# Block 2's mixer: v ahead of lx, masks built earlier, the scale of z moved, GpSimd relieved

## The chip, the cores and the metric

The kernel runs on one core of one Trainium2 chip. The metric is the device time of one execution in microseconds (us). The engines are called PE (TensorE), DVE (VectorE), ACT (ScalarE), POOL (GpSimd) and SP (SyncE, which issues most transfers).

## The reference

Two transformer blocks run one after the other on 256 tokens of 1024 channels in fp32. Block 1 is a hybrid mixer with a mixture of 32 experts. Block 2, which the change is in, has a mixer of a gated linear recurrence (lru) and a gated linear attention (gla), and then a feed-forward part:

```python
h = rms_norm(x, norm1[l]); p = h @ w_in[l]
lru_x, lru_g, q, k, v, g, z = jnp.split(p, SPLIT_IDX, axis=-1)
lru_x = causal_depthwise_conv_2(lru_x, conv_w[l], conv_b[l])      # 4 taps
r = sigmoid(block_diag(lru_x, w_a) + b_a); i = sigmoid(block_diag(lru_x, w_i) + b_i)
log_a = -LRU_C * r * softplus(-lam); a = exp(log_a)
u = sqrt(-expm1(2 * log_a)) * (i * lru_x)                          # then h = a * h + u
lru_o = rg_lru * gelu(lru_g)
log_alpha = log_sigmoid(z @ w_alpha + b_alpha) / GATE_TAU
# chunks of 64: bcum = cumsum(log_alpha); k_dec = k * exp(b_end - bcum)
# q_dec = q * exp(b_end); o = (q @ k_dec^T) @ v + q_dec @ state
gla_o = rms_norm(o, gla_norm) * silu(g)
x = x + concat(lru_o, gla_o) @ w_out
```

Channels: lru_x, lru_g, v and g have 512 each, q and k 256, z 16.

## The kernel before

A matrix product in fp32 is made of three products of rounded halves. A weight tile of 128 by 1024 arrives by DMA (raw); ACT writes its high half (hi), then DVE or POOL subtracts and writes its low half (lo); PE computes high by high, low by high, high by low. Activations are split the same way once.

Block 2's mixer is a list of units, each a weight tile with its 24 products (12 wide ones for v), worked through by `run_units`. For unit i it emits in this order: the actions of `at_pre(i)`, the split of unit i+2, the matmuls of unit i, the action that takes up the result of unit i-1, and the actions of `at(i)`. So each engine's order is fixed by this emission, and each engine works its own list strictly in order. `later(n, f)` puts f at the current unit plus n, `soon` in front of the current unit's actions.

The units are: 0 z, 1 and 2 k, 3 and 4 q, 5 to 8 lru_x (named lx, with the convolution behind it), 9 to 12 v, 13 to 16 lru_g (lg), 17 to 20 g, 21 to 28 the eight row products with w_out. The low halves of units 6 to 14 are made by POOL (`P2`).

The tokens' norm scale (rsb, a row of 256 scales on all partitions) isn't known when the first units begin; their unscaled results wait in PSUM. The sums of squares of h (sh) and of h times gain (g, sum sg) are taken on ACT. At unit `SCALE` a chain of 16 small operations on DVE gives the scale, then dg, a diagonal matrix, and PE multiplies it by ones (rsp) so that ACT can copy rsb. Everything with `from_scale` follows then.

From z come zb (product with w_alpha and bias), its softplus by an exponential and a polynomial of nine steps on DVE (L400), the running sum (`la`), and the decays of k and q (kd, qd). `gate_mm` multiplies a convolved tile xf by the block-diagonal masks wab (built from w_a and w_i), `gate_act` applies the sigmoids (rg, ix) and multiplies ix by xf. `lru_exp` makes al and the tanh from rg, `lru_q` and `lru_u` the input of the recurrence's scan. `k_turn` transposes kd, `scores` and `update` make the score tiles sT and the states st, `attend` the attention output, `gla_norm` its norm, on POOL.

Block 1's weights stream before all this, and the feed-forward part of block 2 follows.

Of the kernel before, what the change touches and what calls it, by code (L numbers as in the profile page):

```python
# [69 lines left out]
def kernel(ctx: ExitStack, tc: tile.TileContext, *aps, dbg=None, stage=9):  # L70
# [154 lines left out]
    def late_loads():  # L225
# [9 lines left out]
        loads += [(wal, A["gla_w_alpha_2"][0]), (wz2, wcols("w_in_2", 2560, 16))]  # L235
# [231 lines left out]
    loads2 = deque([("kq", 1024), ("lx", 0), ("v", 1536), ("lg", 512), ("g", 2048), (("wo", 0), 0), (("wo", 1), 0)])  # L467
# [659 lines left out]
    with ExitStack() as pp:  # L1127
# [317 lines left out]
    with ExitStack() as pc:  # L1445
# [36 lines left out]
        SCALE = 5  # L1482


        wab = [mw.tile([128, 4, 128], F32, name=f"wab{i}", tag=f"wab{i}") for i in range(2)]
        diag = mw.tile([128, 128], F32, name="diag")
        cmask = mw.tile([128, T], F32, name="cmask")

        def masks():
            for t, src_ in zip(wab, (wa2, wi2)):  # L1490
                V.memset(t, 0.0)
                for s in range(2):
                    r = slice(s * 64, (s + 1) * 64)
                    V.tensor_copy(t[r, :, r], src_[r])

        def chunks():
            V.memset(diag, 0.0)
            for s in range(2):
                V.memset(diag[s * 64:(s + 1) * 64, s * 64:(s + 1) * 64], 1.0)
            V.memset(cmask, 1.0)  # L1500
            V.memset(cmask.rearrange("p (c t) -> p c t", c=4)[:, :, 0:1], 0.0)

# [11 lines left out]
        def after_lx(t):  # L1514
            def f(o):
# [17 lines left out]
                later_pre(2, gate_mm, t)  # L1533
# [509 lines left out]
```

## Time and profile before

| | |
|---|---|
| median of three runs | 1029.76 us (1028.13, 1030.2, 1029.76) |
| profiled execution | 1031.31 us, of which span 1029.5 us |
| granted TensorE clock, mean share | 0.911 |
| PE busy | 872.9 us, 85% of the span |
| DVE busy | 433.3 us, 42% |
| ACT busy | 318.8 us, 31% |
| POOL busy | 147.5 us, 14% |
| block 2's mixer | 708.8 to 833.5 us |

The shares are means over stages with different limits. Durations below are those of the one profiled execution; busy PE time at a clock of 0.50 is work that takes half as long at 1.00.

### The profile page before, as it was taken

The numbers are of one execution on the slowest core, as the hardware profiler recorded it, in microseconds if no ns is written. First come the engines' busy times: TensorE is split into PE (matmuls) and PEld (weight loads), VectorE is DVE, ScalarE is ACT, GpSimd is POOL, SyncE is SP. The second block draws the span as 40 slices with busy tenths as digits, with TensorE's granted clock in tenths as the row PEclk, the third lists the DMA queues.
The fourth block names the chain that finished last, engine by engine and source line by source line (L and its number), as shares of the span: only waits on it lengthen the run. The fifth ranks groups of instructions, "written<-read, shape, count | busy, mean of one in ns | idle before, by whom it ended". The sixth has DMA issues, their size and how long they took to land.

```text
span 1029.5 us, 13573 instructions
## 1 busy us (share of the span) xinstructions
PE 872.9 (85%) x5631; PEld 616.6 (60%) x5632; DVE 433.3 (42%) x756; ACT 318.8 (31%) x533; POOL 147.5 (14%) x127
## 2 busy tenths in 40 slices
PE   8999998999868597665858667689679999999997
PEld 8988887777414141321414123136659789999996
DVE  6898565553101110100101010016896776555554
ACT  6665453434001100000000000005446545444444
POOL 4232024002000000000000000002452223111112
PEclk9999998999878778887887878799889999999999
DMA  9594424366999999998999999999725345474301
GB/s 292 135 388 174 164 91 156 96 231 266 393 428 423 427 428 414 427 422 344 429 427 428 427 428 412 428 412 383 273 81 185 102 162 167 164 246 161 126 1 42
DMA packets 77392, 287.85 MB, mean 280 GB/s; under 512 B 12499, under 2 KB 41358, under 8 KB 65678
## 3 DMA queue, kind: packets, MB, share of 16 engines
q1 hardware_dynamic: 76486, 285.03, 71.0%
q0 software_dynamic: 592, 1.60, 0.4%
q8 instruction: 46, 0.75, 0.3%
q10 hardware_dynamic: 248, 0.30, 0.1%
q14 instruction: 20, 0.16, 0.0%
HBM read 285.87 MB, written 1.05 MB: 279 GB/s over the span
## 4 chain that ended last, share of the span: by engine, by line
PE 35%; DMA 10%; DVE 6%; ACT 1%; issue 1%; POOL 0%; DVEq 0%; ACTq 0%; SPq 0%; POOLq 0%
PE p L1185 6%; PE mm L339 5%; PE mm L341 5%; PE mm L340 5%; DMA raw<-in_w_gate_dram 4%; PE py L1211 3%; DMA raw<-in_w_down_dram 3%; PE po L309 3%; PE po L311 3%; PE po L310 3%; PE gp L1168 2%; DMA rawx<-in_w_down_dram 2%; DMA raw<-in_w_up_dram 1%; DVE za L400 1%; DVE xf L1529 1%
## 5 line engine op out<-in xcount | busy, mean ns | idle before, releaser
L339 PE MATMUL mm<-hnh,hi 128*128 128x256 f32 x808 | 233.4, 289 | 1.2 <-ACT cx L702 0.6
L341 PE MATMUL mm<-hnh,lo 128*128 128x256 f32 x808 | 228.6, 283 | 1.4 <-DVE lo L330 1.4
L340 PE MATMUL mm<-hnl,hi 128*128 128x256 f32 x808 | 228.1, 282 | 0.0
L1185 PE MATMUL p<-raw,xse 128*32 128x512 f32 x1008 | 158.1, 678 | 62.8 <-DMA raw<-in_w_gate_dram 57.0
L330 DVE TENSOR_TENSOR lo<-raw,hi 128x1024 fp32r<-128x1024 f32 x137 | 168.9, 1237 | 79.8 <-ACT hi L329 79.8
L329 ACT ACTIVATE hi<-raw 128x1024 fp32r<-128x1024 f32 x152 | 159.1, 1058 | 100.0 <-PE mm L340 39.8
L339 PEld LDWEIGHTS mm<-hnh,hi 128*128 128x128 f32 x808 | 153.6, 190 | 10.6 <-issue 7.5
L341 PEld LDWEIGHTS mm<-hnh,lo 128*128 128x128 f32 x808 | 153.6, 190 | 2.4 <-DVE lo L330 2.2
L340 PEld LDWEIGHTS mm<-hnl,hi 128*128 128x128 f32 x808 | 153.9, 190 | 0.9
L1185 PEld LDWEIGHTS p<-raw,xse 128*32 128x32 f32 x1008 | 36.8, 123 | 172.1 <-issue 85.4
L1211 PE MATMUL py<-raw,hs 128*32 128x512 f32 x496 | 86.4, 719 | 36.3 <-DMA raw<-in_w_down_dram 30.4
L1250 DVE TENSOR_TENSOR h<-h,pc 128x512 f32<-128x512 f32 x32 | 20.5, 683 | 138.2 <-PE pc L1248 138.2
L1211 PEld LDWEIGHTS py<-raw,hs 128*32 128x32 f32 x496 | 19.2, 128 | 95.2 <-DMA raw<-in_w_down_dram 44.5
L1375 POOL TENSOR_TENSOR g<-h,gain 128x512 f32<-128x512 f32 x2 | 3.5, 1779 | 472.3 <-DVE h L1250 472.3
L1168 PE MATMUL gp<-oh,xnf 128*128 128x128 f32 x256 | 65.8, 432 | 4.8 <-ACT xse L1175 4.8
L1168 PEld LDWEIGHTS gp<-oh,xnf 128*128 128x128 f32 x256 | 62.2, 334 | 6.7 <-ACT xse L1175 6.7
L1239 DVE SCALAR_TENSOR_TENSOR lo<-py,gs,hi 128x512 fp32r<-128x512 f32 x14 | 10.5, 751 | 111.5 <-ACT hi L1238 110.8
L1928 POOL TENSOR_TENSOR sgf<-sgf,rsb 128x256 f32<-128x256 f32 x22 | 31.7, 1441 | 134.4 <-ACT sgf L1927 134.4
L1192 ACT ACTIVATE sg<-p 128x512 f32<-128x512 f32 x8 | 4.8, 599 | 146.4 <-PE p L1185 136.0
L330 POOL TENSOR_TENSOR lo<-raw,hi 128x1024 fp32r<-128x1024 f32 x15 | 37.3, 2495 | 40.3 <-ACT hi L329 40.3
L1238 ACT ACTIVATE hi<-py,gs 128x512 fp32r<-128x512 f32 (+1 forms) x15 | 10.1, 673 | 102.5 <-PE py L1211 102.2
L1202 ACT ACTIVATE hs<-p 128x512 f32<-128x512 f32 x8 | 4.8, 597 | 112.7 <-PE p L1200 112.7
(472 smaller groups left out, 1138.3 us busy)
## 6 DMA issues: line engine op xcount, KB each, us to landing
raw<-in_w_gate_dram SPq DMA_DIRECT2D x32, 2048.0 KB
raw<-in_w_up_dram SPq DMA_DIRECT2D x31, 2048.0 KB
raw<-in_w_down_dram SPq DMA_DIRECT2D x28, 2048.0 KB
raw<-in_w_in_dram SPq DMA_DIRECT2D x14, 2048.0 KB
raw<-in_w_ffn_in_dram SPq DMA_DIRECT2D x22, 1024.0 KB
raw<-in_w_out_dram SPq DMA_DIRECT2D x6, 2048.0 KB
raw<-in_w_ffn_out_dram SPq DMA_DIRECT2D x5, 2048.0 KB
raw<-in_w_down_dram SPq DMA_DIRECT2D x12, 512.0 KB
```

Of the source, the lines that this page charges most:

```text
L309: P.matmul(po[a, j], yh[:, ts], wh[:, 0, ns], start=(i == 0), stop=False)
L310: P.matmul(po[a, j], yh[:, ts], wl[:, 0, ns], start=False, stop=False)
L311: P.matmul(po[a, j], yl[:, ts], wh[:, 0, ns], start=False, stop=end)
L329: S.activation(hv[:, r], src[:, r], AF.Copy)
L330: lo_on[0].tensor_tensor(lv, src, hv.bitcast(F32), op=ALU.subtract)
L339: P.matmul(o, wh, xh, start=first, stop=False)
L340: P.matmul(o, wh, xl, start=False, stop=False)
L341: P.matmul(o, wl, xh, start=False, stop=last)
L1168: P.matmul(p[:, kk, :], xn[:, a, 4 * hf + kk::8], OT[g][:, a, :], start=(a == 0), stop=(a == 1))
L1185: P.matmul(p[r], XS[g][:, k, r], ew(4 * g + i, m, k), start=(k == 0), stop=(k == 7))
L1211: P.matmul(PY[g][n][r], HT4[g][:, f, r], ew(4 * g + i, "d", f)[:, n * 512:(n + 1) * 512], start=(f == 0), stop=(f == 3))
L1928: G.tensor_tensor(t, t, rsb, op=ALU.mult)
```

## The change

- The v units come ahead of the lx units, in the loads and in the list: 5 to 8 are v, 9 to 12 lx.
- No low half is made on POOL any more (`P2` is gone). The products ix by xf, the product in `lru_u`, and half of the products h by gain move from POOL to DVE, the square of al to ACT.
- DVE makes the sums of squares of g for the second 128 tokens; ACT scales the rows of h at the end of the scale chain (`rows2_`), which DVE did.
- The masks wab, diag and cmask are built by DVE in `pools2`, during the experts' stage of block 1, in a pool of their own, and not at units 1 and 6.
- z's row scale is applied behind its second product: `after_z` copies 48 rows (high and low parts, w_alpha stacked twice), the product runs at unit 4, and DVE multiplies by rsb when it forms zb. The bias goes into ACT's Abs and is added again in `la`.
- `SCALE` is 6 (was 5), `KT` 14 (was 13), and most actions behind it one unit later. The four `lru_exp` stand at unit 16 together (were two at 14, two at 15), the four scans at 19. The convolved tiles' gates come three units after (was two); the decay's exponentials come one unit after `la` (was two), with the load of the sigmoid's table behind them (it was ahead of the polynomial).

```diff
-P2 = (4, 5, 6, 7, 8, 9, 10, 11, 12)
-KT = 13
+KT = 14
...
-    loads2 = deque([("kq", 1024), ("lx", 0), ("v", 1536), ("lg", 512), ("g", 2048), (("wo", 0), 0), (("wo", 1), 0)])
+    loads2 = deque([("kq", 1024), ("v", 1536), ("lx", 0), ("lg", 512), ("g", 2048), (("wo", 0), 0), (("wo", 1), 0)])
...
                 combine(g, a, n, tag)
-                if not a:
-                    G.tensor_tensor(X2["g"][:, a, ns], h[:, a, ns], gains[1][:, ns], op=ALU.mult)
+                V.tensor_tensor(X2["g"][:, a, ns], h[:, a, ns], gains[1][:, ns], op=ALU.mult)
...
-                V.tensor_scalar(h[:, a, :], X2["g"][:, a, :], y1[:, a:a + 1], None, op0=ALU.mult)
+                S.activation(h[:, a, :], X2["g"][:, a, :], AF.Copy, scale=y1[:, a:a + 1])
...
+        def sums_g1():
             for n in range(2):
-                ns = slice(n * 512, (n + 1) * 512)
-                V.tensor_tensor(X2["g"][:, 1, ns], h[:, 1, ns], gains[1][:, ns], op=ALU.mult)
+                x = X2["g"][:, 1, n * 512:(n + 1) * 512]
+                V.scalar_tensor_tensor(xf.rearrange("p a t -> p (a t)")[:, :512], x, 1.0, x, op0=ALU.mult, op1=ALU.mult,
+                                       accum_out=X2["sg"][:, 1, n:n + 1])
...
-                later_pre(2, gate_mm, t)
+                later_pre(3, gate_mm, t)
...
-            G.tensor_tensor(ix[:, t, :], ix[:, t, :], xf[:, t, :], op=ALU.mult)
+            V.tensor_tensor(ix[:, t, :], ix[:, t, :], xf[:, t, :], op=ALU.mult)
...
-                G.tensor_tensor(s2, al, al, op=ALU.mult)
+                S.activation(s2, al, AF.Square)
...
-            G.tensor_tensor(s2, s2, ix, op=ALU.mult)
+            V.tensor_tensor(s2, s2, ix, op=ALU.mult)
...
         def after_z(o):
-            z1 = za[:16, 0, :]
-            V.tensor_tensor(z1, o[32:48], rsb[32:48], op=ALU.mult)
-            V.tensor_tensor(zs, o[:16], rsb[:16], op=ALU.mult)
-            V.tensor_tensor(zs, zs, z1, op=ALU.add)
-            later_pre(1, zf)
+            S.activation(zs, o[:48], AF.Copy)
...
         def zexp():
+            V.tensor_tensor(zb, Z["p"], rsb[:, None, :].to_broadcast([128, 2, T]), op=ALU.mult)
             for j in range(2):
-                V.tensor_scalar(zb[:, j, :], Z["p"][:, j, :], cols2[:, c_gb + j:c_gb + j + 1], None, op0=ALU.add)
-            S.activation(zu, zb, AF.Abs)
+                S.activation(zu[:, j, :], zb[:, j, :], AF.Abs, bias=cols2[:, c_gb + j:c_gb + j + 1])
             S.activation(zu, zu, AF.Exp, scale=-1.0)
-            S.activation(small.tile([128, 1], F32, name="one"), ones[:, 0:1], AF.Sigmoid)
...
-            later(2, lambda: [S.activation(za, za, AF.Exp, scale=1.0 / 16),
-                              S.activation(eb.unsqueeze(3), be, AF.Exp, scale=1.0 / 16)])
-            later(2, kq_decay)
+            later(1, lambda: [S.activation(za, za, AF.Exp, scale=1.0 / 16),
+                              S.activation(eb.unsqueeze(3), be, AF.Exp, scale=1.0 / 16),
+                              S.activation(small.tile([128, 1], F32, name="one"), ones[:, 0:1], AF.Sigmoid)])
+            later(3, kq_decay)
...
-        units += [col_unit(src2("lx"), t * 128, after_lx(t), tag="mm" if t else "op") for t in range(4)]
         units += [v_unit(i) for i in range(4)]
+        units += [col_unit(src2("lx"), t * 128, after_lx(t)) for t in range(4)]
...
-            at_pre(17 + hd // 2, attend, hd)
+            at_pre(18 + hd // 2, attend, hd)
...
         for t in range(4):
-            at(14 + t // 2, lru_exp, t)
-        at(16, lru_q)
-        at(17, lru_u)
+            at(16, lru_exp, t)
+        at(17, lru_q)
+        at(18, lru_u)
...
-        run_units(units, ready=early2, pool=lambda i: i in P2)
+        run_units(units, ready=early2)
```

Three places of the engines' orders show what the diff doesn't. The first is DVE on the way to the first gate product, which needs xf. Before, from zb on (za by zu is the polynomial; rg is lx times rsb, xf by rg are the convolution's taps):

```order
L1614 TENSOR_SCALAR zb<-tp,cols_141 128x256 x2
L1521 TENSOR_TENSOR rg<-mm,rsb 128x256
L1529 SCALAR_TENSOR_TENSOR xf<-rg,cols_141,xf 128x255
L1529 SCALAR_TENSOR_TENSOR xf<-rg,cols_141,xf 128x254
L1529 SCALAR_TENSOR_TENSOR xf<-rg,cols_141,xf 128x253
L399 TENSOR_SCALAR za<-zu 128x512
L400 SCALAR_TENSOR_TENSOR za<-za,zu 128x512 x3
L1521 TENSOR_TENSOR rg<-mm,rsb 128x256
L1529 SCALAR_TENSOR_TENSOR xf<-rg,cols_141,xf 128x255
L1529 SCALAR_TENSOR_TENSOR xf<-rg,cols_141,xf 128x254
L1529 SCALAR_TENSOR_TENSOR xf<-rg,cols_141,xf 128x253
```

In the changed kernel, from the last polynomial steps to the first convolution (zb, zu and the second za are the running sum of the decay, lo a low half):

```order
L399 SCALAR_TENSOR_TENSOR za<-za,zu 128x512 x3
L329 TENSOR_TENSOR lo<-raw,hi 128x1024
L1517 TENSOR_TENSOR rg<-mm,rsb 128x256
L1621 TENSOR_SCALAR zb<-zb,cols_141 128x256 x2
L1622 TENSOR_TENSOR zb<-zb,za 128x512
L1624 SCALAR_TENSOR_TENSOR zu<-cmask,zb 128x256 x2
L1627 TENSOR_TENSOR za<-zu 128x512
L329 TENSOR_TENSOR lo<-raw,hi 128x1024
L1517 TENSOR_TENSOR rg<-mm,rsb 128x256
L1525 SCALAR_TENSOR_TENSOR xf<-rg,cols_141,xf 128x255
L1525 SCALAR_TENSOR_TENSOR xf<-rg,cols_141,xf 128x254
L1525 SCALAR_TENSOR_TENSOR xf<-rg,cols_141,xf 128x253
```

Before, the first convolution stood ahead of the polynomial and no low half lay in between; now the whole polynomial, the running sum and the low halves of the lx and lg units stand ahead of it.

The second place is ACT between the last convolutions and the gates' sigmoids (rg and ix by tp). Before:

```order
L329 ACTIVATE hi<-raw 128x1024
L1547 ACTIVATE rg<-tp,cols_141 128x256
L1547 ACTIVATE ix<-tp,cols_141 128x256
L329 ACTIVATE hi<-raw 128x1024
L1636 ACT_TABLE_LOAD
L1636 ACTIVATE za<-za 128x512
L1637 ACTIVATE eb<-zu 128x8
L329 ACTIVATE hi<-raw 128x1024
```

In the changed kernel:

```order
L1520 ACTIVATE xf<-rg,cols_141 128x256
L1628 ACTIVATE za<-za 128x512
L1629 ACTIVATE eb<-zu 128x8
L1630 ACT_TABLE_LOAD
L1630 ACTIVATE one<-ones 128x1
L328 ACTIVATE hi<-raw 128x1024
L1520 ACTIVATE xf<-rg,cols_141 128x256
L328 ACTIVATE hi<-raw 128x1024
L1520 ACTIVATE xf<-rg,cols_141 128x256
L1543 ACTIVATE rg<-tp,cols_141 128x256
L1543 ACTIVATE ix<-tp,cols_141 128x256
```

The decay's exponentials (za, eb) stood behind all sigmoids; now they and the load of the sigmoid's table stand ahead of the last two convolutions and of the first sigmoid.

The third place is ACT at the exponentials of the recurrence (al by exp, rg by tanh, s the square). Before:

```order
L329 ACTIVATE hi<-raw 128x1024
L1552 ACTIVATE al<-rg,sp_148 128x256
L1553 ACTIVATE rg<-rg,sp_148 128x256
L1552 ACTIVATE al<-rg,sp_148 128x256
L1553 ACTIVATE rg<-rg,sp_148 128x256
L329 ACTIVATE hi<-raw 128x1024
L1552 ACTIVATE al<-rg,sp_148 128x256
L1553 ACTIVATE rg<-rg,sp_148 128x256
L1552 ACTIVATE al<-rg,sp_148 128x256
L1553 ACTIVATE rg<-rg,sp_148 128x256
L329 ACTIVATE hi<-raw 128x1024 x2
```

In the changed kernel, behind the last gate:

```order
L1543 ACTIVATE rg<-tp,cols_141 128x256
L1543 ACTIVATE ix<-tp,cols_141 128x256
L1548 ACT_TABLE_LOAD
L1548 ACTIVATE al<-rg,sp_149 128x256
L1549 ACTIVATE rg<-rg,sp_149 128x256
L1548 ACTIVATE al<-rg,sp_149 128x256
L1549 ACTIVATE rg<-rg,sp_149 128x256
L1548 ACTIVATE al<-rg,sp_149 128x256
L1549 ACTIVATE rg<-rg,sp_149 128x256
L1548 ACTIVATE al<-rg,sp_149 128x256
L1549 ACTIVATE rg<-rg,sp_149 128x256
L1551 ACTIVATE s_4853<-al 128x1024
```

The eight stood in two groups with a high half between; now they stand in one group, behind a table load, with the square and the next high half after them.

## Rows read from the trace of the kernel before

**Rows 1.** Windows: length, busy PE, PEld, DVE, ACT, POOL (x count), clock, DMA, GB/s

```profile
724.00:732.00 8.00, 0.01 (x1) 0.00 (x0) 7.48 (x20) 0.00 (x0) 4.89 (x3) 0.65 1.04 399
732.00:736.70 4.70, 4.64 (x20) 4.46 (x21) 3.90 (x10) 1.33 (x2) 1.97 (x1) 0.50 0.24 95
...
748.30:754.20 5.90, 0.00 (x0) 0.00 (x1) 5.83 (x5) 2.27 (x4) 5.50 (x3) 0.67 0.00 0
754.20:757.20 3.00, 2.97 (x7) 2.45 (x8) 2.90 (x6) 0.69 (x2) 0.00 (x0) 0.51 0.00 0
...
771.20:786.60 15.40, 15.40 (x141) 14.07 (x139) 11.37 (x19) 10.80 (x15) 3.32 (x3) 1.00 0.62 206
786.60:806.30 19.70, 19.70 (x149) 17.28 (x148) 11.40 (x23) 7.83 (x12) 4.68 (x7) 1.00 0.30 107
```

**Rows 2.** PE's waits, 700 to 830: total us, times, longest

```profile
PE rsp L290 <- DVE dg L286: 8.0, 1, 8.0
PE tp L1542 <- DVE xf L1529: 7.3, 2, 5.9
PE mm L341 <- DVE lo L330: 0.9, 2, 0.5
PE tp L1785 <- POOL n L257: 0.4, 1, 0.4
```

**Rows 3.** Timeline of DVE, 708 to 738: start us, us, engine, line, operation

```profile
711.60 1.28 DVE L1250 TENSOR_TENSOR h<-h,pc 128x512 f32<-128x512 f32 x2
712.79 1.95 DVE L330 TENSOR_TENSOR lo<-raw,hi 128x1024 fp32r<-128x1024 f32 x1
...
724.42 2.18 DVE L1456 TENSOR_TENSOR w<-sh 128x2 f32<-128x2 f32 x1
...
726.64 2.27 DVE L1458 TENSOR_SCALAR w<-w 128x2 f32<-128x2 f32 x1
...
729.15 0.16 DVE L1460 SCALAR_TENSOR_TENSOR w<-w,w 128x2 f32<-128x2 f32 x1
...
731.52 0.48 DVE L286 TENSOR_SCALAR dg<-ident,w 128x128 f32<-128x128 f32 x2
```

**Rows 4.** Timeline of DVE, 742 to 773

```profile
742.14 1.51 DVE L1529 SCALAR_TENSOR_TENSOR xf<-rg,cols,xf 128x255 f32<-128x255 f32 x3
...
748.51 5.57 DVE L1529 SCALAR_TENSOR_TENSOR xf<-rg,cols,xf 128x255 f32<-128x255 f32 x3
754.00 2.13 DVE L400 SCALAR_TENSOR_TENSOR za<-za,zu 128x512 f32<-128x512 f32 x3
...
765.00 1.27 DVE L1632 TENSOR_TENSOR_SCAN zu<-cmask,zb 128x256 f32<-128x256 f32 x2
...
770.95 1.21 DVE L330 TENSOR_TENSOR lo<-raw,hi 128x1024 fp32r<-128x1024 f32 x1
772.08 0.68 DVE L386 COPY kdt<-tp 128x512 f32<-128x512 f32 x1
```

**Rows 5.** Groups by line, 708 to 834: busy us, mean ns, idle before

```profile
L330 POOL TENSOR_TENSOR lo<-raw,hi 128x1024 fp32r<-128x1024 f32 x9 | 22.9, 2561 | 17.0 <-ACT hi L329 17.0
```

**Rows 6.** Timeline of ACT, 760 to 786

```profile
767.51 1.28 ACT L1636 ACT_TABLE_LOAD   x1
...
771.84 1.05 ACT L329 ACTIVATE hi<-raw 128x1024 fp32r<-128x1024 f32 x1
772.79 0.50 ACT L1552 ACTIVATE al<-rg,sp 128x256 f32<-128x256 f32 x1
```

**Rows 7.** Chain that ended last, 764 to 776, PE's pieces: start us, us, what

```profile
764.51 1.10 PE tp L1542 x4
...
771.22 0.43 PE tp L1660 x4
...
772.30 0.32 PE mm L339
...
775.33 0.65 PE sc L1716 x8
```

More of the change, by code (lines that the diff above doesn't have):

```diff
@@ L234, in late_loads @@
                   for t, nm in ((wa2, "lru_wa_2"), (wi2, "lru_wi_2")) for s in range(2)]
-        loads += [(wal, A["gla_w_alpha_2"][0]), (wz2, wcols("w_in_2", 2560, 16))]
+        loads += [(wal[r:r + 16], A["gla_w_alpha_2"][0]) for r in (0, 32)] + [(wz2, wcols("w_in_2", 2560, 16))]
         for t, ap in loads:
@@ L1335, in pools2 @@
             hn = ctx.enter_context(tc.tile_pool(name="hn", bufs=1, side="right", reuse_waits="tile"))
+            X2["masks"] = ExitStack()
+            bm = X2["bm"] = X2["masks"].enter_context(tc.tile_pool(name="bm", bufs=1, side="right", reuse_waits="tile"))
             X2["pool"] = ExitStack()
@@ L1341, in pools2 @@
             X2["sh"], X2["sg"] = [small.tile([128, 2, 2], F32, name=f"s{i}") for i in "hg"]
+            X2["wab"] = [bm.tile([128, 4, 128], F32, name=f"wab{i}", tag=f"wab{i}") for i in range(2)]
+            for t, src_ in zip(X2["wab"], (wa2, wi2)):
+                V.memset(t, 0.0)
+                for s in range(2):
+                    r = slice(s * 64, (s + 1) * 64)
+                    V.tensor_copy(t[r, :, r], src_[r])
+            diag = X2["diag"] = bm.tile([128, 128], F32, name="diag")
+            cmask = X2["cmask"] = bm.tile([128, T], F32, name="cmask")
+            V.memset(diag, 0.0)
+            for s in range(2):
+                V.memset(diag[s * 64:(s + 1) * 64, s * 64:(s + 1) * 64], 1.0)
+            V.memset(cmask, 1.0)
+            V.memset(cmask.rearrange("p (c t) -> p c t", c=4)[:, :, 0:1], 0.0)
         HT = []
@@ L1480, in buf @@
             return mw.tile([128, 4, T], dt, name=name, tag=tag or name)
[L1482 to L1501, printed above, removed]
+        SCALE = 6
+        bm = X2["bm"]
+        wab, diag, cmask = X2["wab"], X2["diag"], X2["cmask"]
         xf, rg, ix = [buf(n) for n in ("xf", "rg", "ix")]
@@ L1629, in la @@
         def la():
-            V.scalar_tensor_tensor(zb, zb, 0.0, za, op0=ALU.min, op1=ALU.subtract)
+            for j in range(2):
+                V.tensor_scalar(zb[:, j, :], zb[:, j, :], cols2[:, c_gb + j:c_gb + j + 1], 0.0, op0=ALU.add, op1=ALU.min)
+            V.tensor_tensor(zb, zb, za, op=ALU.subtract)
             for j in range(2):
@@ L1856 @@
         at_pre(KT, k_turn)
-        at_pre(KT, scores, 0)
-        at_pre(14, scores, 1)
+        for c in range(2):
+            at_pre(KT + c, scores, c)
         for c in range(3):
-            at_pre(14 + c, update, c)
+            at_pre(KT + 1 + c, update, c)
         for hd in range(4):
-            at_pre(17 + hd // 2, attend, hd)
-        at(19, gla_norm0)
-        at_pre(20, gla_norm1)
-        at_pre(22, gla_norm2)
+            at_pre(18 + hd // 2, attend, hd)
+        at(20, gla_norm0)
+        at_pre(21, gla_norm1)
+        at_pre(23, gla_norm2)
         at(21, g_silu)
@@ L1868 @@
         for i in range(2):
[L1869 to L1870 removed]
+            at_pre(24, gla_scale, i)
+            at(24, gla_split, i)
         for t in range(4):
[L1872 to L1874 removed]
+            at(16, lru_exp, t)
+        at(17, lru_q)
+        at(18, lru_u)
         for t in range(4):
[L1876 to L1877 removed]
+            at(19, lru_scan, t)
+            at(20 + t // 2, lru_out, t)
             at(20 + t // 2, lru_lo, t)
         at(18, lru_gelu)
[L1880 to L1889 removed]
+        at(0, sums2, h, "sh", 1)
+        at(0, sums_g1)
+        at(1, sums2, X2["g"], "sg", 0)
+        at(3, scales2)
+        at(4, load_next2)
+        at_pre(4, zf)
+        at(SCALE, zexp)
+        at_pre(SCALE, lambda: across_mm(dg, rsb, ps.tile([128, T], F32, name="rsp", tag="ss")))
+        at(4, rows2_)
         at(GAINS, lambda: gains.extend([gain_rows("norm2_2", nc.gpsimd), gain_rows("final_norm_2", nc.gpsimd)]))
```

43 lines of the change are left out of this document (11 added, 32 removed).

## The prediction

> **What bounds the kernel now.** The windows come first [rows 1]. Only the mixer section of block 2, which begins at 708.8 us and hands over to the feed-forward part at 833.5, is touched in earnest, so everything is read there. TensorE (PE) is busy for 15.40 of 15.4 us between 771.2 and 786.6, and for all of the next 19.7, at a granted clock of 1.00. Two windows stand out against these: 724 to 732, with 0.01 us of PE, and 748.3 to 754.2, with none. Behind each of them comes a stretch in which PE is full but the granted clock is 0.50 and 0.51, its lower level of 1.2 GHz: 4.64 us and 2.97 us of work that would take half of that at 2.4. So each hole costs twice: 8.0 and then about 2.3; 5.9 and then about 1.5.
>
> The view of PE's waits names who is late [rows 2]. One wait of 8.0 us is for dg, the diagonal matrix of row scales from VectorE (DVE). Two waits of 7.3 in all are for xf, the convolved channels, also from DVE. 0.9 is for the low halves of weights at the start and 0.4 for POOL's norm chain at the first row products. With the two clock losses that is 8.0 + 7.3 + 0.9 + 0.4 + 2.3 + 1.5 = 20.4 us that PE loses in this section. The sum below replaces this number by another. DMA isn't the limit after 732: its share there is 0.00 to 0.62 [rows 1].
>
> Why DVE is late shows in its timeline [rows 3, 4]. The three taps of a convolution take 1.51 us at 742.14 and 5.57 at 748.51. In the slow stretch of 748.3 to 754.2 POOL was busy for 5.50 of 5.9 us, and from 754.2 to 757.2, where three steps of the polynomial take 2.13, for nothing [rows 1, 4]. POOL's work is above all nine low halves at 2.56 us each [rows 5]. Beside POOL, DVE thus runs at a third of its speed.
>
> **The change, part by part.** Rule for chains: an instruction on ACT or DVE starts about 0.1 us before the end shown of the one ahead of it (the high half is 1.05 long and its follower starts 0.95 later [rows 6]; the low half 1.21 and 1.13 [rows 4]). All positions are those of before, shifted by what is found on the way.
>
> *Taken off POOL.* DVE takes back nine low halves (9 x 1.13 = 10.2 us), four products ix by xf (half of the 0.68 for 512 columns [rows 4], so 4 x 0.34), one of 1024 columns (1.1), two gain products and two sums (4 x 0.65), and gives the masks to a place before 708.8 and two row scalings to ACT. In exchange its own instructions cost what they cost alone. The trace can't say how much of the slowing goes; between none (below, it isn't likely) and all I take all, since the quick rows are those beside an idle POOL.
>
> *The wait for dg.* Without masks ahead of it the scale chain is 16 small operations at 0.2 us (twelve starts from 729.15 to the one ahead of 731.52 [rows 3]), 3.2, and dg 0.5. It follows the low halves of q's second unit and v's first, done at about 724.1: dg stands at 727.8. PE now asks for it one unit later, after v's first unit. By then PE is at 724.0 + 2.3 (start, next part) + 0.9 (z's second product, moved forward, priced by a gate's 1.10 of the same shape [rows 7] less the overlap) + 2.8 (v's unit: two of them fill 765.61 to 771.22 [rows 7]) = 730.0. There are 2.2 us to spare. **The 8.0 and its 2.3 vanish.**
>
> *The start.* On DVE the order is now low half, then h, g, h, g, and again. h and g are 0.60 to 0.68 [rows 3], so k's second low half begins 1.3 later, at 714.2, and ends at 715.4 where it ended at 714.7 [rows 3]: PE waits 1.0. The fourth sum on ACT needs the fourth h, which stands behind that low half (717.1); q's first high half comes behind the sum at 718.9, where PE wants it at 717.9: 1.1 more, and its low half again 1.2. That makes 3.3 for 0.9 before, so +2.4. Bounds: nothing (if ACT slips the high half ahead) and 4.
>
> *v ahead of lx.* Three v units (8.4) end at 738.9, four lx units (11.3) and two short waits for their accumulators, 1.2 together because the first scaling of lx on DVE is late, end at 751.4.
>
> *The first gate.* The row scale reaches SBUF at 731.6, zb follows at 733.3, two absolute values, the table load of 1.28 [rows 6], the exponential and a high half bring 737.1. From there DVE has in order: five low halves 5.7, the polynomial 0.4 + 9 x 0.72 = 6.9, two scalings 0.7, the decay's five pieces 3.2 (the two scans are 1.27 of it [rows 4]), one convolution 1.5: 18.0, so 755.0. PE waits 755.0 - 751.4 = **3.6, new**. Bounds: the nine steps at 0.68 and each low half at 1.10 give 3.1; a third more on each step, if some of the slowing stays, gives 5.8.
>
> *k_turn.* The turned k needs kd, which DVE now computes behind the first gate's ix. On ACT the order is exponentials, the sigmoid's table load, a high half, further convolutions, sigmoids. From the first gate's 753.4 on: ACT 0.5 + 0.6 + 1.4 + 1.1 brings 757.1; DVE's low half, scaling, convolution, low half, scaling (1.13 + 0.34 + 1.5 + 1.13 + 0.34) 761.5; ACT's xf and two sigmoids of some 0.45 each 762.9; ix and kd 1.0: 763.9. PE has the gate and one lg unit (3.0 [rows 7]) and at full clock would be there at 759.1: **4.8, new**; a clock loss of the gate's wait lies inside it. Bounds 3.4 and 6.
>
> *scores and attend.* After k_turn the second scores wait 0.8 for their buffer on DVE. Then the bundle that stands at unit 16 on ACT: two sigmoids 0.9, a table load 1.3, eight exponentials and tanhs at 0.50 each, less overlap, 3.8 [rows 6], a square 1.0, a high half 1.1; then on DVE low half, scaling, lru_q and the last state, 1.2 + 0.3 + 1.1 + 0.6. From the fourth gate that is 11.2; PE has two units and some products for 7.7 (3.0 + 0.65 + 3.0 + 1). The wait is **3.5, new**, with bounds 2 and 4.5. Before, the same eight lay two by two between units, in ACT's idle time, and nobody waited.
>
> Three of the changed kernel's six table loads lie in these three chains, at the trace's 1.28 each [rows 6]. The Trainium skill, ScalarE: Activation LUTs, section "Table sets: the hidden batching unit", gives about 2.7 us for a load and advises to batch activations by set. With the page's figure each of the three waits would be 1.4 longer and the whole 4.2, at 1033.7; the measured row decides.
>
> *The clock.* In this trace it fell after waits of 8.0 and 5.9, not after 0.4 to 1.4. The new ones of 3.5 to 4.8 lie between. They are nearer to 5.9, so I take a loss of 1.5 behind the second and third: 3.0 (bounds 0 and 4.6).
>
> *Norm.* The norm chain on POOL gets a second row unit as cover: the 0.4 goes. Loads in the other order, the doubled z weights, and the masks in the experts' stage cost nothing: that stage waits for weights, and DVE is idle there.
>
> Sum of losses: 3.3 + 1.2 + 3.6 + 4.8 + 0.8 + 3.5 + 3.0 = 20.2 for 20.4. The change is -0.2: against the profiled execution of 1031.31, 1031.1; that run is 1.55 above the median of 1029.76, so the forecast as a median is **1029.5**. About 0.2%, 2.1 us, is what a measurement of this kernel can tell from no change.
>
> **Rivals.**
> *A, faster: the clock holds through the new waits.* Then the 3.0 go: -3.2, 1026.5; and if the chains of DVE and ACT ahead of the three waits (18, 10.5 and 11.2 us) are 5% shorter than my prices, another 2, or 1024.5. For it: no wait as short as these is seen to lower the clock [rows 2]. Against: PE falls to half within 8 us of idleness already [rows 1]. The Trainium skill, TensorE: Matmul & The Clock Gate, section "HAM oscillation — how this bites in real kernels", says that a kernel whose matmuls stop for data again and again pays the slow clock each time anew; that speaks against this rival, and no run here shows it for waits of this length.
>
> *B, slower: the clock falls at shorter waits than before showed.* The start now has three waits within 8 us (1.0, 1.1, 1.2); if they bring 1.2 GHz, q's units take up to 2.3 more, and since dg then is no longer awaited, PE pays it all; behind the two later waits 2.3 each stand for 1.5. That is 2.3 + 1.6 - 0.2 = +3.7, 1033.5. It decides once the granted clock between 717 and 727 is under 0.8. Against: with 0.9 of such waits the clock stayed.
>
> *C, the wait for dg stays.* If the first and third of the small operations keep their 2.2 us [rows 3] (they were slow beside POOL), dg comes at 731.9, PE waits 1.9: 1031.4 and no change. POOL has nothing there, so this is unlikely.
>
> **How the numbers follow.** Forecast 0.36, A 0.36, B 0.24, C 0.04. Faster by over 0.2% is A, 0.36; same is the forecast and C, 0.40; slower is B, 0.24. The range runs from 1023.0 (A with shorter chains, and the start's waits at their lower bound) to B's 1033.5. The likeliest case alone has 1027.5 to 1031.5: its bounds at the three new waits don't add up, as a later first gate takes from the second.
>
> **What would show it.** No PE wait for dg, granted clock 1.00 from 727 to 751; a PE wait of 3 to 4 us for xf near 751, one of 3.5 to 5 for kd before the turned k, one of 3 to 4 for the state at the first attention products; POOL all but idle from 709 to 800, and each step of the polynomial near 0.7. Wrong it would be if the polynomial's steps stay over 0.9 (the first gate then comes 2 or more later), or if the three waits shrink under 2 each, which would make it faster by 4 to 6.

## The result, and the profile after

The changed kernel takes 1035.39 us in the median (1033.49 to 1036.7, five runs); its ratio to the kernel before is 1.0057 [1.0041, 1.0073]. It is slower by 0.57%, and the time lies above the range that was forecast (1023.0 to 1033.5). Its profiled execution took 1036.09 us, with a span of 1034.3: 4.8 more than before.

Two marks in the trace share the 4.8 out. Block 2's mixer begins with the first product of z, at 711.15 us where it was 708.83: **2.3 us are lost in block 1**, where the forecast had nothing. From there to the first product of the feed-forward part it is 127.2 us where it was 124.6: **2.6 are lost in the mixer**. The feed-forward part is the same, 196.0 in both.

The two marks, in the kernel before and then in the changed kernel:

```profile
708.83 0.28 PE L627 MATMUL mm<-hnh,hi 128*48 128x256 f32 x1
...
833.47 0.39 PE L339 MATMUL mm<-hnh,hi 128*128 128x256 f32 x1
```

```profile
711.15 0.28 PE L626 MATMUL mm<-hnh,hi 128*48 128x256 f32 x1
...
838.35 0.38 PE L338 MATMUL mm<-hnh,hi 128*128 128x256 f32 x1
```

In the mixer, PE's waits of the changed kernel, 690 to 845 us (total, times, longest):

```profile
PE tp L1648 <- DVE kd L1634: 5.5, 1, 5.5
PE op L1737 <- DVE st L1692: 3.7, 1, 3.7
PE tp L1538 <- DVE xf L1525: 3.1, 1, 3.1
PE mm L340 <- DVE lo L329: 2.1, 3, 0.9
...
PE mm L338 <- ACT hi L328: 0.8, 1, 0.8
PE mm L338 <- DVE rg L1517: 0.8, 1, 0.8
```

The wait for dg [rows 2] is gone, and the waits of new origin are there: the first gate (xf), the turned k (kd), the states (st), and short ones at the start (lo, hi) and at lx's accumulators (rg). They sum to 16.0. DVE's timeline shows why dg is no longer late: its small operations take 0.16 each, and dg is written at 729.4 to 729.8, where it ended at 732 before [rows 3].

```profile
728.96 0.16 DVE L245 TENSOR_TENSOR w<-w,w 128x4 f32<-128x4 f32 x1
729.16 0.16 DVE L246 SCALAR_TENSOR_TENSOR w<-w,w 128x4 f32<-128x4 f32 x1
729.36 0.48 DVE L285 TENSOR_SCALAR dg<-ident,w 128x128 f32<-128x128 f32 x2
```

What follows the waits is in the windows of the changed kernel (length, busy PE, PEld, DVE, ACT, POOL, granted clock, DMA share, GB/s):

```profile
711.15:727.00 15.85, 12.87 (x95) 11.13 (x94) 13.82 (x25) 10.86 (x21) 0.53 (x1) 1.00 1.05 388
757.00:761.10 4.10, 3.81 (x28) 3.65 (x28) 1.78 (x4) 2.46 (x4) 0.00 (x0) 1.00 0.28 88
761.10:766.60 5.50, 0.12 (x2) 0.00 (x0) 3.85 (x8) 3.79 (x6) 0.00 (x0) 0.92 0.00 0
766.60:772.00 5.40, 5.32 (x22) 4.41 (x23) 3.53 (x8) 0.94 (x3) 0.00 (x0) 0.50 0.18 47
...
788.80:792.60 3.80, 0.39 (x4) 0.25 (x3) 2.72 (x4) 3.28 (x4) 0.00 (x0) 1.00 0.00 0
792.60:800.00 7.40, 7.11 (x31) 6.66 (x32) 5.19 (x8) 4.89 (x6) 0.00 (x0) 0.54 0.61 210
800.00:811.60 11.60, 11.60 (x85) 9.57 (x84) 6.86 (x13) 3.96 (x8) 0.00 (x0) 1.00 0.12 48
```

Behind the wait for kd PE is full for 5.3 us at a clock of 0.50, which loses 2.7; behind the wait for the states 7.1 at 0.54, which loses 3.3; 0.3 more lie in the 16.8 us between these windows, at 0.98. That is 6.3 for the 3.0 of the forecast. POOL is idle in all these windows but one.

The other loss stands in block 1. First the one wait between 245 and 290 us that grew, PE's first for the experts' down weights, in the changed kernel and then in the kernel before:

```profile
PE py L1210 <- DMA raw<-in_w_down_dram: 3.5, 1, 3.5
```

```profile
PE py L1211 <- DMA raw<-in_w_down_dram: 2.0, 1, 2.0
```

Then POOL's timeline, in the changed kernel all of it from 255 to 730 us (in brackets the idle time before), and in the kernel before where the same two loads stood:

```profile
261.01 0.53 POOL L116 DMA_DIRECT2D gain<-in_norm_dram  x1 [19.44 <-POOLq L1254]
720.74 0.53 POOL L116 DMA_DIRECT2D gain<-in_final_norm_dram  x1 [459.19 <-DVE g L1388]
```

```profile
777.73 2.25 POOL L1555 TENSOR_TENSOR s<-al 128x1024 f32<-128x1024 f32 x1 [10.13 <-ACT al L1552]
779.93 0.60 POOL L118 DMA_DIRECT2D gain<-in_norm_dram  x1
780.52 0.53 POOL L118 DMA_DIRECT2D gain<-in_final_norm_dram  x1
```

These two executions don't show the whole 2.3 behind that load, though. At an earlier load of gains in block 1, 20 us ahead of it, the changed kernel is already 1.5 late; from there to the mixer it takes 470.2 us, the kernel before 469.4. Again the changed kernel and then the kernel before:

```profile
240.96 0.62 POOL L116 DMA_DIRECT2D gain<-in_final_norm_dram  x1
```

```profile
239.48 0.62 POOL L118 DMA_DIRECT2D gain<-in_final_norm_dram  x1
```

Unit 15 of the mixer asks POOL to load two rows of gains onto all partitions, 512 KB each. Before, low halves and products stood ahead of them in POOL's list. In the changed kernel nothing does, so the first goes out 519 us earlier, into the stream of the experts' weights. Whether that is what block 1 lost, and what the parts of the change are worth in the mixer, is what the experiments ask.

### The profile page after: what moved, and what is told of

Read it like the earlier page. It is cut to its first block, busy times and chain, and to the rows that moved or that the text cites. A ratio compares the mean times of both kernels' runs of the same rounds, so it can differ in the third digit from the quotient of the medians.

```text
span 1034.3 us, 13555 instructions
## 1 busy us (share of the span) xinstructions
PE 880.7 (85%) x5631; PEld 621.6 (60%) x5632; DVE 429.0 (41%) x772; ACT 320.6 (31%) x534; POOL 114.0 (11%) x111
## 4 chain that ended last, share of the span: by engine, by line
PE 34%; DMA 10%; DVE 5%; ACT 3%; issue 2%; DVEq 0%; ACTq 0%; SPq 0%
PE p L1184 6%; PE mm L338 4%; PE mm L340 4%; PE mm L339 4%; DMA raw<-in_w_gate_dram 4%; PE po L308 3%; PE po L310 3%; DMA raw<-in_w_down_dram 3%; PE po L309 3%; PE py L1210 3%; PE gp L1167 2%; DMA rawx<-in_w_down_dram 2%; DMA raw<-in_w_up_dram 1%; DVE lo L329 1%; ACT hi L328 1%
## 5 line engine op out<-in xcount | busy, mean ns | idle before, releaser
L329 DVE TENSOR_TENSOR lo<-raw,hi 128x1024 fp32r<-128x1024 f32 x146 | 178.9, 1230 | 92.5 <-ACT hi L328 92.5
L1210 PE MATMUL py<-raw,hs 128*32 128x512 f32 x496 | 89.6, 738 | 35.2 <-DMA raw<-in_w_down_dram 29.2
L1237 ACT ACTIVATE hi<-py,gs 128x512 fp32r<-128x512 f32 (+1 forms) x15 | 10.1, 674 | 104.6 <-PE py L1210 104.3
L310 PE MATMUL po<-hi,al 128*128 128x512 f32 x88 | 34.9, 397 | 0.0
```

The costliest lines, as they stand in the source:

```text
L310: P.matmul(po[a, j], yl[:, ts], wh[:, 0, ns], start=False, stop=end)
L329: lo_on[0].tensor_tensor(lv, src, hv.bitcast(F32), op=ALU.subtract)
L1210: P.matmul(PY[g][n][r], HT4[g][:, f, r], ew(4 * g + i, "d", f)[:, n * 512:(n + 1) * 512], start=(f == 0), stop=(f == 3))
```

## The experiments

The table has every kernel that ran: the ratio to the kernel before with its interval, the start of the mixer, its length up to the feed-forward part, and PE's first wait for down weights. The kernel before ran beside each of them; its medians were 1029.07 to 1031.27 us, so ratios are compared, not times. The last three columns come from one profiled execution each, and they scatter: three kernels with the mixer of the changed kernel (changed, e1, e5) read 127.2 to 127.6, three with the mixer of before (before, e2, e6) 123.8 to 125.2. A difference of less than 1.5 in that column shows nothing by itself.

| kernel | ratio | start | mixer | down wait |
|---|---|---|---|---|
| before | 1 | 708.8 | 124.6 | 2.0 |
| changed kernel | 1.0057 [1.0041, 1.0073] | 711.2 | 127.2 | 3.5 |
| e1 changed, one w_alpha load | 1.0046 [1.0031, 1.0060] | 711.0 | 127.3 | 3.1 |
| e2 before, two w_alpha loads | 1.0009 [0.9995, 1.0024] | 708.1 | 125.2 | 2.0 |
| e5 changed, gain loads held | 1.0018 [0.9997, 1.0038] | 706.9 | 127.6 | 1.7 |
| e6 before, gain load early | 1.0012 [0.9994, 1.0030] | 708.6 | 123.8 | 3.9 |
| e3 changed, kd a unit earlier | 1.0048 [1.0030, 1.0065] | 709.9 | 126.8 | 3.5 |
| e11 e5, exponentials a unit later | 1.0022 [1.0005, 1.0038] | 709.8 | 127.7 | 2.1 |
| e14 e5, idle products | 1.0050 [1.0033, 1.0067] | 708.8 | 129.3 | 2.0 |
| e15 e5, idle products that fill the waits | 0.9999 [0.9984, 1.0013] | 708.6 | 123.9 | 1.5 |
| e12 e5, lx ahead of v again | 0.9959 [0.9945, 0.9973] | 706.4 | 120.3 | 1.9 |
| e4 before, masks early | 0.9982 [0.9968, 0.9997] | 708.0 | 122.9 | 2.1 |
| e9 e4, low halves on POOL from unit 10 | 0.9976 [0.9959, 0.9993] | 707.5 | 123.6 | 2.1 |
| e10 e4, no low halves on POOL | 0.9935 [0.9912, 0.9959] | 708.2 | 118.5 | 1.2 |
| e13 e10, z's scale behind its second product | 0.9963 [0.9949, 0.9977] | 708.3 | 120.6 | 2.1 |

**Block 1: which of the loads?** The change also loads w_alpha twice, on SP, ahead of the weights. That was the first theory.

```diff
-        loads += [(wal[r:r + 16], A["gla_w_alpha_2"][0]) for r in (0, 32)] + [(wz2, wcols("w_in_2", 2560, 16))]
+        loads += [(wal[:16], A["gla_w_alpha_2"][0]), (wz2, wcols("w_in_2", 2560, 16))]
...
+            V.tensor_copy(wal[32:48], wal[:16])
```

> The changed kernel with w_alpha loaded once and its second copy made by DVE in the experts' stage. Theory P: in the changed kernel the second small load holds up SyncE's queue ahead of the weights of block 1 (its next weight issue stands at 42.9 us, before at 38.4), and block 2 starts 2.3 us later (711.15 for 708.83) for that reason; then block 2 starts near 709.0 to 710.0 here and the whole takes 1033.4 or less (ratio to before 1.0015 to 1.0040). Theory Q: the 2.3 us are scatter of the stream from run to run; then the whole stays at 1034.5 to 1036.

The counterpart is the kernel before with `wal` of 48 rows loaded twice (e2), of which only the first 16 are used.

```diff
-        loads += [(wal, A["gla_w_alpha_2"][0]), (wz2, wcols("w_in_2", 2560, 16))]
+        loads += [(wal[r:r + 16], A["gla_w_alpha_2"][0]) for r in (0, 32)] + [(wz2, wcols("w_in_2", 2560, 16))]
```

> The kernel before with w_alpha loaded twice into a tile of 48 rows (the second copy isn't used). Theory P: block 2 starts 1 to 2.3 us later, at 710 to 711, and the whole takes 1031 to 1032 (ratio 1.001 to 1.002). Theory Q: nothing changes beyond 0.1%.

SP's next weight load moved as it should, to 39.19 us from 42.86 in e1 and to 42.81 from 38.44 in e2, but the mixer still began at 711.0 in e1 and at 708.1 in e2. The second w_alpha load costs nothing that shows, and the theory falls. Then the gain load: an operation on POOL that needs the row scale, and whose result nobody reads, stands ahead of it (e5).

```diff
+        at(GAINS, lambda: G.tensor_tensor(zs, rsb[:48], rsb[:48], op=ALU.mult))
```

> The changed kernel with one small POOL operation on the row scale ahead of the two loads of gain rows, so that POOL can't issue them before some 733 us. Theory G: with POOL's list emptied, the load of 512 KB of norm gains that stood at 779.9 us in before goes out at 261 us, in the middle of the experts' weights, which then come late (the first down weights are waited for 3.5 us and not 2.0); block 2 begins 2.3 us later for that reason alone. Then block 2 begins at 708.0 to 709.3 here and the whole is 2 to 2.8 us under the changed kernel: 1032.5 to 1033.4 (ratio to before 1.002 to 1.0035). Rival: the late start of block 2 has another cause; then 711 and 1034.8 or more stay.

POOL's timeline in e5:

```profile
731.04 0.59 POOL L116 DMA_DIRECT2D gain<-in_norm_dram  x1
731.63 0.53 POOL L116 DMA_DIRECT2D gain<-in_final_norm_dram  x1
```

The down wait fell to 1.7, the ratio to 1.0018, the mixer stayed at 127.6. The counterpart puts that load early into the kernel before (e6).

```diff
+            gains.append(gain_rows("norm2_2", nc.gpsimd))
...
-        at(GAINS, lambda: gains.extend([gain_rows("norm2_2", nc.gpsimd), gain_rows("final_norm_2", nc.gpsimd)]))
+        at(GAINS, lambda: gains.append(gain_rows("final_norm_2", nc.gpsimd)))
```

> The kernel before with only that load of gain rows moved on POOL's list ahead of the products h by gain, so that it goes out at about 261 us. Theory G: block 2 begins 1.5 to 2.5 us later (709.8 to 711), the whole takes 1032 to 1032.8 (ratio 1.0015 to 1.003). Rival: 512 KB are 1.2 us of the stream at most and are made up later; then 1030 to 1031.

The down wait rose to 3.9, but the mixer began at 708.6 and the ratio's interval holds 1: the local effect is shown, the whole one not by this run. All kernels together say more. The four with the load at 259 to 261 us have down waits of 3.1 to 3.9 and begin the mixer at 710.2 on average (708.6 to 711.2); the eleven with it late have 1.2 to 2.1 and 708.1 (706.4 to 709.8). Part of that is scatter from ahead of the load. Counted from block 1's earlier load of gains, at 238.3 to 241.0 us, the four take 469.4 to 471.3 to the mixer (470.4 on average), the eleven 467.5 to 471.5 (468.7); e6 and the kernel before both take 469.4. So the early load costs about 1.7 us of the start on average, and single executions of the two kinds overlap. The size is plausible: at the 427 GB/s of the changed kernel from 350 to 450 us, 512 KB are 1.2 us of the stream (an estimate). The ratios of the changed kernel and of e5 differ by 0.0039, which is 4 us, with intervals that just miss each other.

**The mixer: one wait at a time.** e3 takes kd out of the way.

```diff
-            later(3, kq_decay)
+            later(2, kq_decay)
```

> The changed kernel with the decayed k and q (kd, qd) emitted one unit earlier, so that on DVE they stand ahead of the first ix instead of behind it. Theory K: the wait of 5.5 us for kd is made by what stands ahead of kd on DVE and ACT, not by its own inputs (the decay's exponential is done at 756.8, kd begins at 765.9); then the wait falls to 0.5 to 1.5, the products behind it start 4 us earlier and the whole takes 1030.5 to 1032. Rival: what is saved there comes back as a longer wait at the second gate, the scores or the states; then 1033.5 or more.

PE's longest waits in e3:

```profile
PE op L1737 <- DVE st L1692: 3.7, 1, 3.7
PE tp L1538 <- DVE xf L1525: 3.2, 1, 3.2
PE tp L1538 <- ACT ix L1543: 2.7, 1, 2.7
...
PE sc L1704 <- DVE sT L1705: 1.8, 1, 1.8
```

The 5.5 for kd is gone and the turned k comes 3.8 earlier, but ix and sT are awaited instead, and the mixer is 0.4 shorter, which is within the scatter: the saved time came back at the next consumers of the same DVE and ACT chain. e11 moves the exponentials off the way to the states (with the gain load held).

```diff
-            at(16, lru_exp, t)
-        at(17, lru_q)
+            at(17, lru_exp, t)
+        at(18, lru_q)
...
-        at(18, lru_gelu)
+        at(19, lru_gelu)
```

> The changed kernel with the gain loads held, and the eight exponentials and tanhs with the square at unit 17 (lru_q at 18, gelu at 19) in place of 16. Theory L: the wait of 3.7 us for the state and the slow clock behind it (7.1 us busy at 0.54, so 3.3 lost) are made by that bundle on ACT; one unit later it stands behind the high half that the chain needs, both go, and of 1032.3 some 4 to 7 us go: 1025.5 to 1028.5. Rival: the bundle then holds up the squares of the attention output or the recurrence ahead of the row products, and gives back what it saves: 1030.5 or more.

No wait for st is left, but there is one for og of 2.4, and the mixer is 127.7 against 127.6: given back in full.

**The clock's own price.** e14 and e15 put products whose result nobody reads into PE's three waits. In e14:

```diff
+        at_pre(13, keep_warm, ps, 8, "tp")
+        at_pre(KT, keep_warm, ps, 12, "tp")
...
+        at_pre(18, keep_warm, ps, 8, "tp")
```

> The changed kernel with the gain loads held and idle products of ones put ahead of the three waits (8 ahead of the first gate, 12 ahead of the turned k, 8 ahead of the first attention products; some 2.1, 3.2 and 2.1 us at full clock, less than each wait). Theory H: the slow clock behind the waits is a cost of its own, 5.5 to 6.3 us in all; with PE busy it stays at 1.00 and the mixer falls from 127.6 to 121.5 to 123.5, the whole from 1032.3 to 1026.5 to 1028.5. Rival: the waits grow by what the clock gives back, as VectorE's and ScalarE's chains set the time; then 1031 or more.

It didn't settle the question, because the third group had to wait for its own accumulator:

```profile
PE warm L296 <- DVE st L1692: 5.1, 1, 5.1
PE tp L1648 <- DVE kd L1634: 2.9, 1, 2.9
```

One thing it does show: with the first group the clock is 1.00 from 753 to 760 where e5 had 0.50 from 753 to 757, and the turned k still comes 55.6 us into the mixer (55.5 in e5). What the clock costs behind the first gate lies inside the wait for kd, as the prediction had it. e15 makes the groups 12, 24 and 14 long and gives the third a free accumulator (`"tq"`).

> The changed kernel with the gain load held, and idle products put into PE's three waits at such lengths that they fill them (12, 24 and 14 small products: about 2.9, 5.7 and 3.4 us at full clock), the third in a buffer that nobody holds, so that it starts when PE falls idle. The kernel with the load held and no such products has a mixer of 127.6 us, with the clock at 0.77 for 7.3 us behind the wait for kd and at 0.50 for 7.5 us behind the wait for the state. Theory K (the clock behind the two later waits is paid on the path): the clock stays at or above 0.95 from 753 to 800, and the mixer shortens by the two losses less some overshoot of the products, 4 to 5, to 122.5 to 124; time about 1028 to 1029. Rival (the chain of DVE and ACT that reaches the row products sets the end, or the products themselves are in the way): the clock stays high and the mixer remains at 126 or more, with new waits for sT, og or the norm; time 1031 to 1034.

Windows of e15:

```profile
751.00:786.00 35.00, 33.60 (x279) 31.34 (x278) 21.20 (x40) 19.34 (x32) 0.29 (x1) 1.00 0.33 107
786.00:790.00 4.00, 3.45 (x27) 3.00 (x26) 4.00 (x7) 3.46 (x4) 0.00 (x0) 1.00 0.00 0
790.00:794.00 4.00, 4.00 (x22) 3.93 (x22) 3.01 (x5) 3.14 (x5) 0.00 (x0) 0.57 0.75 220
794.00:824.00 30.00, 30.00 (x164) 23.64 (x164) 21.51 (x34) 14.38 (x21) 8.52 (x15) 1.00 0.32 112
```

With the waits filled, the clock holds but for 4 us (4.0 x 0.43 = 1.7 lost), and the mixer is 123.9, 3.7 shorter than in e5. The turned k stands at 55.6 again. But the last state is written earlier, counted from the start of the mixer. The four operations that update the states, with the times at which the first and the last of them start, in e5 and then in e15:

```profile
L1692 DVE SCALAR_TENSOR_TENSOR st<-st,eb,tp x4: 342/342/343, 778.6 to 788.2; 128x128 f32<-128x128 f32 x4
```

```profile
L1692 DVE SCALAR_TENSOR_TENSOR st<-st,eb,tp x4: 342/342/343, 778.8 to 788.4; 128x128 f32<-128x128 f32 x4
```

The last one stands 81.3 us into the mixer in e5 and 79.8 in e15. So the clock behind the two later waits was paid on the path: about 1.5 of the 3.7 up to the states, the rest behind them. The ratio fell from 1.0018 to 0.9999; these intervals overlap, the marks carry the reading.

**The parts alone.** e4 builds the masks early in the kernel before and changes nothing else: the bodies of `masks` and `chunks` move into `pools2`.

```diff
+            X2["masks"] = ExitStack()
+            bm = X2["bm"] = X2["masks"].enter_context(tc.tile_pool(name="bm", bufs=1, side="right", reuse_waits="tile"))
...
-        at(1, masks)
-        at(6, chunks)
+        X2["masks"].close()
```

> The kernel before with one part of the change alone: the masks are built in the experts' stage. My reading of before: the two mask copies stand ahead of the scale chain on DVE until 724.4, its sums are done at 720.8, so the wait for dg falls from 8.0 by about 3.5 to 4.5 us, the rest stays; 1025 to 1026.5 (ratio 0.995 to 0.997). Rival: the chain's small operations then run beside POOL's low halves and cost as much as they did (2.2 us each for the slow ones); then less than 1.5 us is gained, 1028 or more.

DVE's timeline in e4, and POOL's beside it:

```profile
720.88 0.17 DVE L243 TENSOR_SCALAR w<-w 128x4 int32<-128x4 int32 x1
721.09 2.34 DVE L245 SCALAR_TENSOR_TENSOR w<-w 128x4 f32<-128x4 f32 x1
723.46 2.26 DVE L246 TENSOR_TENSOR w<-w,w 128x4 f32<-128x4 f32 x1
725.75 2.26 DVE L247 SCALAR_TENSOR_TENSOR w<-w,w 128x4 f32<-128x4 f32 x1
728.05 0.16 DVE L245 SCALAR_TENSOR_TENSOR w<-w 128x4 f32<-128x4 f32 x1
```

```profile
721.00 7.00 POOL L330 TENSOR_TENSOR lo<-raw,hi 128x1024 fp32r<-128x1024 f32 x3 [1.29 <-ACT hi L329]
```

The scale chain is free of the masks, but three of its operations last as long as a low half on POOL each (7.00 / 3 = 2.33), from POOL's start to its end; dg is awaited for 6.6 still. e9 takes units 6 to 9 from POOL as well (`P2` is counted two units ahead), e10 all.

```diff
-P2 = (4, 5, 6, 7, 8, 9, 10, 11, 12)
+P2 = (8, 9, 10, 11, 12)
```

> The kernel before with the masks in the experts' stage, and POOL making the low halves of the units from 10 on only (P2 from 8), so that no low half of POOL runs beside the scale chain. Masks alone left a wait of 6.6 us for dg, since three operations of two columns took 2.3 us each beside POOL's low halves. Theory C: the chain then takes 3.2 us from 720 on and dg is there at 724, the wait falls to 0 to 1.5 us, with the slow clock behind it gone: 1020 to 1023 (ratio 0.990 to 0.9935). Rival: DVE's four more low halves (4.5 us) push the first convolutions and come back as a longer wait for xf (6.0 now); then 1025 or more.

```diff
-P2 = (4, 5, 6, 7, 8, 9, 10, 11, 12)
+P2 = ()
```

> The kernel before with the masks in the experts' stage and no low half on POOL (P2 empty); order of units, scale of z, exponentials and loads as before. Theory C and the exchange as in the sum on record: DVE's own work shrinks by some 17 us and grows by 10, the wait for dg goes, that for xf shrinks from 6.0 to 1 to 3: 1018 to 1022. Rival: emptying POOL costs DVE more than it gives once the masks are away from the chain; then 1025 or more, and what made the changed kernel slow is the low halves, not the order of the units.

In e9 the wait for dg is 0.4, but zs is awaited for 3.2 and xf for 7.3, and the mixer is no shorter than e4's. PE's waits in e10, 705 to 835 us:

```profile
PE tp L1542 <- ACT hi L329: 3.3, 1, 3.3
PE tp L1542 <- DVE xf L1529: 3.1, 2, 1.7
PE tp L1609 <- DVE zs L1603: 2.1, 1, 2.1
...
PE rsp L290 <- DVE dg L286: 0.2, 1, 0.2
```

The mixer is 118.5: **6.1 shorter than before**, and at 0.9935 this kernel beats both. e13 adds the new treatment of z to e10.

```diff
+            S.activation(zs, o[:48], AF.Copy)
...
-        units = [narrow_unit(lambda: wz2, from_scale(after_z), tag="ss")]
+        units = [narrow_unit(lambda: wz2, after_z, tag="ss")]
...
+        at_pre(3, zf)
+        at(SCALE, zexp)
```

> The kernel before with early masks, no low halves on POOL, and now z's row scale behind its second product. Theory Z: the wait of 2.1 us for zs behind the row scale goes and the polynomial begins earlier; 1021.5 to 1023.5 (ratio 0.9905 to 0.9935). Rival: PE's next wait for the convolutions takes it up; then 1024 to 1025.5.

The wait for zs is gone, but the wait for hi rises from 3.3 to 4.6, that for xf from 3.1 to 4.3, one of 1.8 for kd is new, and the mixer is 2.1 longer, which neither expectation had. The intervals of the two ratios overlap, so the 2.1 rests on one execution of each. Last, e12 puts lx ahead of v again in the changed kernel with the gain load held.

```diff
-    loads2 = deque([("kq", 1024), ("v", 1536), ("lx", 0), ("lg", 512), ("g", 2048), (("wo", 0), 0), (("wo", 1), 0)])
+    loads2 = deque([("kq", 1024), ("lx", 0), ("v", 1536), ("lg", 512), ("g", 2048), (("wo", 0), 0), (("wo", 1), 0)])
...
-        SCALE = 6
+        SCALE = 5
...
+        units += [col_unit(src2("lx"), t * 128, after_lx(t), tag="mm" if t else "op") for t in range(4)]
         units += [v_unit(i) for i in range(4)]
-        units += [col_unit(src2("lx"), t * 128, after_lx(t)) for t in range(4)]
```

> The changed kernel with the gain loads held and the lx units ahead of the v units again (in the list and the loads, SCALE 5); everything else as changed. Theory O: it is the order of the units that costs the mixer its 8.7 us against the kernel with early masks and no low halves on POOL (118.5 us from z to the feed-forward part, here 127.6), since v ahead of lx leaves the convolutions no time; then the first gate stands at 33 to 37 us from the start, the mixer takes 118 to 122 and the whole 1023 to 1027. Rival B: the bundle of exponentials and the sigmoid's later table load cost more than the order; then the mixer stays over 124.5 and the whole at 1029.5 or more.

PE's waits in e12:

```profile
PE tp L1538 <- ACT ix L1543: 7.3, 1, 7.3
PE mm L340 <- DVE lo L329: 2.2, 3, 0.9
PE tp L1538 <- ACT hi L328: 1.8, 1, 1.8
```

The first gate comes 34.2 us into the mixer instead of 46.1, the waits for xf, kd and st are gone, one of 7.3 for ix is new, and the mixer is 7.3 shorter (120.3 for 127.6), at 0.9959. The parts add up: 118.5 (masks and low halves) + 2.1 (z) + 7.3 (v first) = 127.9, and e5, which has them all, has 127.6. The other edits, such as the exponentials in one group and the products taken from POOL, come to -0.3 together by this sum; alone they were not tried.

## Why the prediction was wrong

**The step that failed** is the sentence that the loads and the masks in the experts' stage cost nothing. The second w_alpha load and the masks do cost nothing there (e1, e4); the load that it did not name is the gain row on POOL's list. It followed the work that leaves POOL, but not the transfers that were queued behind that work. The first of them moves by 519 us, and block 1 pays about 1.7 us for it on average, as the way from 240 us to the mixer and the down wait show; in the two executions compared above it is 0.8, and the other 1.5 of their 2.3 were there before the load. That part alone takes a forecast of no change to the edge of what can be measured.

**The term that was mis-sized** is the clock: 3.0 taken, 6.3 lost behind the two waits, of which e15 gives 3.7 back against e5. I priced the loss by the stretch behind the wait of 5.9 before, 1.5; behind waits of 5.5 and 3.7 it was 2.7 and 3.3. The upper bound of the forecast, 4.6, was too low as well.

**What held.** The wait for dg and its clock loss went. The new waits came where they were put and in size: start 2.9 (3.3 forecast), lx's accumulators 0.8 (1.2), first gate 3.1 (3.6), k_turn 5.5 (4.8), states 3.7 (3.5), scores none (0.8): 16.0 for 17.2. A step of the polynomial takes 0.69 (nine in 6.2 us), near the 0.72 taken from start to start; the mean before was 1.20. The size of the wait for kd owes something to luck: the clock stayed at 1.00 behind the first gate, and where it fell there, in e1 and e5, the same turned k was awaited for 2.8 and 2.6. With the clock the losses are 22.3, for 20.4 before: +1.9 of the mixer's +2.6. The other 0.7 is no wait: PE's busy time, with the slow stretches counted at full clock, is 104.3 for 103.7. I can't place it.

**Sums that don't come out.** The pieces of the bundle at unit 16 add up to 11.3 (11.2 was written), the lower end of the range to 1024.5 - 2.4 = 1022.1 (1023.0), and the chain to kd is counted from a first gate at 753.4, where its own sum has 755.0. None of these decides the outcome.

**The rivals.** A is false: the clock did not hold. The Trainium skill, TensorE: Matmul & The Clock Gate, section "HAM oscillation — how this bites in real kernels", says that a kernel whose matmuls stop for data again and again pays for the slow clock each time; the trace agrees for two of the three later stops, with 0.50 and 0.54 behind kd and the states, and not for the first gate's, with 1.00 behind it. B's place is false: the granted clock from 711 to 727 was 1.00; that the clock falls behind waits shorter than 5.9 is right, but it did so at the two later waits and not at the start. C is false, with no wait for dg; its fear was not idle, since e4 shows three small operations of the chain at 2.3 when POOL does work beside them.

**Why the gain did not come.** Taking the low halves from POOL and building the masks early are worth 6 us (e10). The rest takes back more than that: v ahead of lx delays the first gate by 12 us, and with it the chain of DVE and ACT up to the states (7.3, e12); the later scale of z costs 2.1 in the one pair of executions that shows it (e13). Moving one link of that chain changes who is awaited, not the end (e3, e11). Not tried is the best mix, such as e10 with part of the later edits.

## What to carry to other kernels

Work that leaves an engine's list also releases every transfer queued behind it: look up what stands there, and when it would go out with nothing ahead. An edit that frees an engine is worth its whole gain only when the order does not make its chain start later; time the two apart. A wait of 4 to 6 us can cost from half of it to nearly as much again in clock (2.7 behind 5.5, 3.3 behind 3.7): price it by the stretch behind it, not by the longest wait seen so far.

## What was not expected of the hardware

- The granted clock fell to 0.50 behind waits of 5.5 and 2.9 us (the second in e14, for kd) and to 0.54 behind one of 3.7. Behind the first gate's wait of 3.1 it stayed at 1.00 in the changed kernel, and behind the same wait of 3.1 in e5 it was 0.50 from 753 to 757. The length of the wait alone does not decide it; what does stays open.
- DVE operations on four columns took 2.3 us beside POOL's subtractions of 1024, for 0.16 alone; three of them filled the 7.00 us of three subtractions (e4). The Trainium skill, SBUF — State Buffer, section "SBUF: two separate sides", says that the port pair which these two engines share is an exclusive lock: the first takes it for its whole instruction and the other waits, on VectorE's side if its operation reads two SBUF inputs or runs in a two-port mode. The three rows agree in their length.
- The load of 512 KB on POOL's queue landed 12.2 us after its issue beside the weights (400 GB/s from 261 to 274 us in the changed kernel), and 5.0 us after it in the mixer before. PE's wait for the weights that come on SP's queue grew with it, to 3.1 to 3.9. The load in the changed kernel and in the kernel before (size, us to landing):

```profile
gain<-in_norm_dram POOLq DMA_DIRECT2D x1, 512.0 KB, 12.2
```

```profile
gain<-in_norm_dram POOLq DMA_DIRECT2D x1, 512.0 KB, 5.0
```
